# A two-layer hybrid decoder: the low weight parts of the mixers on GpSimd, the convolution's square root used once as a square, the key halves duplicated by DMA

## The chip, the core and the metric

The kernel runs on one core of a Trainium2 chip. The time is the device time of one execution in microseconds (us). Engines are named as the profile does: PE is TensorE's matmul, PEld its weight load, DVE is VectorE, ACT is ScalarE, POOL is GpSimd, and SP is SyncE, which here issues every DMA.

## The reference

Two layers over x of 1024 tokens by 1024 channels, all in float32. What matters of it:

```python
for l in range(DEPTH):                       # 2
    h = rmsnorm(x, attn_norm[l])
    proj = h @ w_in[l]                       # 1024 x 1952
    (c_q, c_kv, k_r, g_b, g_c, u_conv, u_pool, q_sw, k_sw, v_sw) = jnp.split(proj, pts, axis=-1)
    y_a = mla_attention(...)                 # latent attention, 4 heads, causal
    y_b = short_gated_conv(g_b, g_c, u_conv, conv_w[l])   # g_b * conv3(g_c * u)
    y_c = multiscale_pool(u_pool, pool_w[l], pool_scale[l])
    y_d = swa_sink_attention(...)            # window 128, 4 heads on 2 key heads
    groups = jnp.stack([y_a, y_b, y_c, y_d], axis=2)      # each scaled to unit mean square
    ...
    x = x + mixed @ w_o[l]
    h2 = rmsnorm(x, ffn_norm[l])
    gate, up = jnp.split(h2 @ w_gate_up[l], 2, axis=-1)
    x = x + (jax.nn.silu(gate) * up) @ w_down[l]
return rmsnorm(x, final_norm)
```

## The kernel before

Activations lie transposed in SBUF: 128 channels on the partitions, 512 tokens (one of two halves, `t`) along a row. A float32 product is made of matmuls in `fp32r`: each operand is split into a high part, a cast that ACT makes, and a low part, the operand minus its high part, which DVE makes; then high times high, high times low and low times high are summed in PSUM (`mm3`, L260). So each weight tile that is loaded costs an ACT cast and a DVE subtraction before PE can use it.

The first stage of a layer is the mixers. `expect_layer` lists the weights in the order of their use: 15 column tiles of `w_in` (1024 columns each; in layer 0 three of them are made elsewhere), a narrow one for the rotary key, and 8 tiles of `w_o` (768 columns). `weights` loads one (L194), casts it (L202) and subtracts (L203), into a ring of two pairs of slots; `ahead` and `take` keep one set fetched. The narrow weights of the latent attention (128 or 256 columns) go through the same function with buffers of their own (`vraw`, `vhi`, `vlo`). `project` takes a set and makes both halves of one column tile of the input projection. The root-mean-square norm is not applied to the input of the projection but to its output: every product leaves PSUM multiplied by `r_of(t)`, the reciprocal root of the mean square, by `mul_to` (L359 whatever calls it).

The convolution (`conv`) takes three projections for each of two channel tiles: `u` and `g_c`, whose product `z` is filtered with three taps on ACT and DVE (L711, L713), and `g_b`, which gates the result. The windowed attention holds each key head twice, on partitions 0 to 63 and 64 to 127, with a high and a low tile each (`kk`), because the low part of a query lies in the other half of the partitions; L539 to L542 make them, and L573 are the first matmuls that read them. Its sixteen units (`swa_unit`) are laid between the projections by `swa_some`. In the latent attention `mix_values` transposes probabilities (L1032) and multiplies them with the values (L1044); the last block of a diagonal needs a strip of zeros that GpSimd clears (L1041). In the mixers GpSimd makes only those clears and 8 additions a layer for feed-forward weights (`premake`, L749 to L752).

After the mixers come the output projection (`out_part`, `out_last`), the entrance to the feed-forward part (`combine`, the splits of the first gate weights, L283), 22 steps of gate and up, and the down projection. There GpSimd makes sums of weights (L1213 to L1243, L1532) and the product of the gate (L1454).

The order of instructions on every engine is not that of the code. `Order` takes the traced program with a cost for each instruction and plans it by list scheduling, forth and back; `impose` then fixes each engine's order, and the planned ends choose the eight PSUM banks. Its rule on DVE and GpSimd stands in `run`: an instruction of DVE with two wide inputs in SBUF is stretched by `SHARED` = 0.6 of what it overlaps with GpSimd's, and the other way round.

Of the kernel before, what the change touches and what calls it, by code (L numbers as in the profile page):

```python
# [14 lines left out]
AF = mybir.ActivationFunctionType  # L15
ALU = mybir.AluOpType
AX = mybir.AxisListType

P = 128
# [92 lines left out]
def trunk_kernel(ctx: ExitStack, tc: tile.TileContext, ins, out, given=None):  # L112
    nc = tc.nc
    act, dve, pe, pool, sp = nc.scalar, nc.vector, nc.tensor, nc.gpsimd, nc.sync
# [9 lines left out]
    R, F = View(slots, F32R), View(slots, F32)  # L124

    def rd(ap):
        return ap.bitcast(F32)
# [42 lines left out]
    def tmp(tag="te"):  # L170
        return tpool.tile([P, HT], F32, name=tag, tag=tag, bufs={"te": 2, "tn": 3, "tp": 3}[tag])
# [7 lines left out]
    def ring_next():  # L179

        if len(ring) == 2:
            ring_drop()
        ring.append((R.pair(), R.pair()))
        return ring[-1]
# [5 lines left out]
    def weights(src, n):  # L190
        if n > 2 * P:
            s = F.pair()
            raw = F.ap2(s)
            sp.dma_start(raw[:, :n], src)  # L194
            hi, lo = (R.ap2(i) for i in ring_next())
            F.free_pair(s)
        else:
            raw = wpool.tile([P, 2 * P], F32, name="vraw", tag="vraw")
            sp.dma_start(raw[:, :n], src)
            hi = wpool.tile([P, 2 * P], F32R, name="vhi", tag="vhi")  # L200
            lo = wpool.tile([P, 2 * P], F32R, name="vlo", tag="vlo")
        act.copy(hi[:, :n], raw[:, :n])  # L202
        dve.tensor_tensor(out=lo[:, :n], in0=raw[:, :n], in1=rd(hi[:, :n]), op=ALU.subtract)  # L203
        return hi, lo

    def rope_weights(l):
# [17 lines left out]
    def expect_layer(l):  # L224
        for m in (2, 3, 0, 4, 5, 6, 1, 13, 14, 10, 11, 12, None, 7, 8, 9):
            if m is None:
                expect(rope_weights, l)
            else:
                if l or m not in (2, 3, 0):
                    expect(weights, ins["w_in"][l, m], 2 * HT)  # L230
        for d in range(NK):
            expect(weights, ins["w_o"][l, d, :, 2 * P :], 6 * P)
# [58 lines left out]
    def half_split(f, gain=None):  # L291
        h, l = R.half(), R.half()
        split(R.ap(h), R.ap(l), f, gain)
        return h, l
# [63 lines left out]
    def mul_to(o, a, b):  # L358
        dve.tensor_tensor(out=o, in0=a, in1=b, op=ALU.mult)  # L359

    def pcol(l, c, rows=slice(0, P)):
        return par[rows, l * PC_N + c : l * PC_N + c + 1]
# [55 lines left out]
    for l in range(L):  # L418
# [20 lines left out]
        def project():  # L439
            w = take()  # L440
            pp = [proj(w, t) for t in range(2)]
            ahead()
            return pp

        def r_of(t):
            return F.ap(ratt[t])
# [26 lines left out]
        if l == 0:  # L473
# [12 lines left out]
            raw = F.pair()  # L486
# [22 lines left out]
            for i in range(L):  # L509
                for o, c, n in ((nsink, PC_SINK, 4), (nffn, PC_FFN, NK)):  # L510
                    dve.tensor_scalar(
                        out=o[:, i * n : i * n + n],
                        in0=par[:, i * PC_N + c : i * PC_N + c + n],
# [20 lines left out]
        for t in range(2):  # L534
            f = tmp()
            mul_to(f, pk[t], r_of(t))
            for g, own, oth in ((0, hd, tl), (1, tl, hd)):
                k1, k2 = R.ap(kk[g][0] + t), R.ap(kk[g][1] + t)
                act.copy(k1[own], f[own])  # L539
                act.copy(k1[oth], f[own])  # L540
                dve.tensor_tensor(out=k2[own], in0=f[own], in1=rd(k1[own]), op=ALU.subtract)
                dve.tensor_tensor(out=k2[oth], in0=f[own], in1=rd(k1[own]), op=ALU.subtract)  # L542
        vs = [[R.half(), R.half()] for _ in range(2)]
        for t in range(2):
            f = tmp()
# [5 lines left out]
            for g in range(2):  # L551
# [3 lines left out]
                    out=o[:, :, 1, :], in0=pv[:, :, g, :], in1=rd(o[:, :, 0, :]), op=ALU.subtract  # L555
# [140 lines left out]
        def conv(ct):  # L696

            z = F.pair()
            pp = project()
            for t in range(2):  # L700
                mul_to(F.ap(z + t), pp[t], r_of(t))
            yield
            pp = project()
            for t in range(2):
                f = tmp()
                mul_to(f, pp[t], r_of(t))
                mul_to(F.ap(z + t), F.ap(z + t), f)
            ac = F.pair()
            zf, af = F.ap2(z), F.ap2(ac)
            c = PC_CONV + ct  # L710
            act.activation(af, zf, AF.Copy, scale=pcol(l, c + 4))  # L711
            for lag, tap in ((1, c + 2), (2, c)):
                dve.scalar_tensor_tensor(  # L713
                    out=af[:, lag:],
                    in0=zf[:, : S - lag],
                    scalar=pcol(l, tap),
                    in1=af[:, lag:],
                    op0=ALU.mult,
                    op1=ALU.add,
                )  # L720
            F.free_pair(z)
            yield
            pp = project()
            for t in range(2):
                f = tmp()
                mul_to(f, pp[t], r_of(t))
                mul_to(F.ap(ac + t), F.ap(ac + t), f)
            y["b"][ct] = [ac, ac + 1]
            yield

        for _ in conv(0):
            swa_some(3)
# [5 lines left out]
        raw = wpool.tile([P, 2 * P], F32, name="vraw", tag="vraw")  # L738
# [23 lines left out]
        for ct in range(2):  # L762
            pp = nextp
# [17 lines left out]
            else:  # L781
# [7 lines left out]
                out=dst,  # L789
                in0=src,  # L790
                scalar=cst[:, CC_INVW + ct : CC_INVW + ct + 1],
                in1=uf,
# [8 lines left out]
            for t in range(2):  # L801
                h, lo = half_split(dst[:, t * HT : (t + 1) * HT])
# [20 lines left out]
        for m in range(2):  # L823
            pp = project() if m else nextp
            for t in range(2):
                f = tmp()
# [6 lines left out]
        pp = project()  # L833
# [12 lines left out]
        for t in range(2):  # L846
# [14 lines left out]
            f = tmp()  # L861
# [24 lines left out]
        def values():  # L886

            wv = weights(ins["w_ukv"][l, :, 2 * P :], 2 * P)
            for jj in range(4):
                va[jj] = [R.half(), R.half()]  # L890
# [428 lines left out]
        def snap(p):  # L1319
            o = tmp("tn")  # L1320
            act.copy(o, p)  # L1321
            return o
# [12 lines left out]
        steps = ((0, 0), (0, 1), (1, 0), (1, 1), (2, 0), (2, 1), (3, 1), (3, 0))  # L1335
        pieces = (0, 3, 2, 3, 1, 1, 1, 1)
        conv1 = conv(1)
        next(conv1)
        group_scale("d")
# [276 lines left out]
        for f in range(3, NFF):  # L1616
# [22 lines left out]
            k2 = snap(w.pa)  # L1639
# [96 lines left out]
        for n, (c, m) in enumerate(units):  # L1736
            if n + 2 < len(units):
                raws.append(dn_raw(*units[n + 2]))
            if c in fresh:
                u, t = fresh[c]  # L1740
# [460 lines left out]
```

## Time and profile before

| | |
|---|---|
| median of 3 runs | 2062.73 us (2062.2 to 2065.04) |
| span of the profiled execution | 2061.2 us |
| instructions in it | 26597 |
| granted clock of TensorE | 0.998 |
| busy share of the span: PE, PEld, DVE, ACT, POOL | 99%, 81%, 73%, 48%, 28% |

The profile gives the span, from the first to the last instruction, of one execution; no device time of its own stands beside it. The median of the runs is 1.5 us above that span. The mixers take from the start to about 350 us and from about 1075 to 1375 us, the gate and up steps from about 475 and 1490 us, the down projections from about 820 and 1840 us. In the views, a row of instructions names line, engine, operation, the tiles written and read (buffer numbers left out), their shapes and how many there are; then the busy time, the mean of one in ns, and the idle time of the engine ahead of it with what ended it. In a timeline the first two numbers are the start and the length in us. Slots are all named `u`.

### The profile page before, as it was taken

The page shows a single profiled execution, that of the slowest core. Times are in us where ns is not written, and L with a number is a line of the kernel's source. Part 1 is how long each engine was busy: PE and PEld are TensorE (multiplying, and loading weights), DVE is VectorE, ACT ScalarE, POOL GpSimd, SP SyncE. Part 2 cuts the span into 40 slices and gives each one's busy share as a digit, 9 for nine tenths or more (in the row PEclk, how much of TensorE's full clock was granted, in tenths as well). Part 3 has the DMA queues.
Part 4 walks back from the last instruction along what each step waited for, and adds up shares of the span by engine and source line. Part 5 has one row for each costly group of instructions (what it writes and reads, how often), then busy time and mean ns, then how long its engine had stood idle before and what let it go on. Part 6 is the DMA issues. An engine that isn't in the chain of part 4 may idle for free.

```text
span 2061.2 us, 26597 instructions
## 1 busy us (share of the span) xinstructions
PE 2035.3 (99%) x9422; PEld 1673.6 (81%) x9422; DVE 1503.7 (73%) x2443; ACT 992.6 (48%) x1743; POOL 577.3 (28%) x420
## 2 busy tenths in 40 slices
PE   9999999999999999999999999999999999999998
PEld 7887888778888888888888878888788877788887
DVE  8779979987666667655657898889866655585555
ACT  7447657753333334444433666668433333354342
POOL 0200000037777773000002000000577777710000
PEclk9999999999999999999999999999999999999999
DMA  5211223334554556766413112142455555487642
GB/s 191 90 57 46 84 78 96 137 133 168 181 175 167 189 169 235 265 220 208 140 46 124 37 42 97 61 144 94 159 169 178 178 175 170 154 302 237 204 171 96
DMA packets 142118, 302.37 MB, mean 147 GB/s; under 512 B 13856, under 2 KB 60960, under 8 KB 141984
## 3 DMA queue, kind: packets, MB, share of 16 engines
q1 hardware_dynamic: 141984, 300.66, 43.1%
q8 instruction: 74, 1.21, 0.2%
q14 instruction: 60, 0.49, 0.1%
HBM read 212.00 MB, written 87.56 MB: 145 GB/s over the span
## 4 chain that ended last, share of the span: by engine, by line
PE 68%; POOL 7%; DVE 5%; DMA 4%; issue 2%; ACT 2%; SPq 0%; DVEq 0%; POOLq 0%; ACTq 0%
PE ps_mm L260 25%; PE ps_s L260 21%; PE ps_t L260 8%; PE ps_pv L260 6%; POOL u L1532 3%; PE ps_pv L1044 2%; PE ps_t L1032 1%; DMA u<-in_w_dn 1%; POOL tp L1454 1%; DMA ad<-u 1%; POOL u L1214 1%; DVE u L283 1%; POOL u L1213 1%; ACT u L280 1%; DMA u<-in_w_gu 1%
## 5 line engine op out<-in xcount | busy, mean ns | idle before, releaser
L260 PE MATMUL ps_mm<-u,u 128*128 128x512 f32 (+1 forms) x3378 | 831.0, 390 | 3.4 <-ACT u L280 2.3
L260 PEld LDWEIGHTS ps_mm<-u,u 128*128 128x128 f32 x3378 | 615.4, 188 | 130.4 <-issue 5.3
L260 PE MATMUL ps_s<-u,u 128*128 128x512 f32 x2670 | 636.1, 390 | 5.8 <-DVE tn L352 2.3
L283 DVE TENSOR_TENSOR u<-u,u 128x1024 fp32r<-128x1024 f32 (+2 forms) x400 | 443.3, 1126 | 225.2 <-ACT u L280 173.4
L260 PEld LDWEIGHTS ps_s<-u,u 128*128 128x128 f32 x2670 | 499.5, 188 | 117.8 <-ACT tn L1321 3.9
L280 ACT CAST u<-u 128x1024 fp32r<-128x1024 f32 (+2 forms) x400 | 345.1, 881 | 505.4 <-POOL u L1215 60.1
L260 PE MATMUL ps_t<-u,u 128*128 128x512 f32 (+1 forms) x1124 | 255.3, 378 | 2.8 <-DVE u L1447 2.7
L260 PEld LDWEIGHTS ps_t<-u,u 128*128 128x128 f32 x1124 | 201.6, 188 | 45.8 <-DVE u L1447 6.5
L1454 POOL TENSOR_TENSOR tp<-tp,u 128x512 f32<-128x512 f32 x80 | 135.1, 1689 | 341.7 <-ACT tp L1453 341.7
L260 PE MATMUL ps_pv<-u,u 128*128 128x512 f32 x744 | 177.8, 390 | 1.6 <-DVE te L1658 1.0
L260 PEld LDWEIGHTS ps_pv<-u,u 128*128 128x128 f32 x744 | 139.3, 188 | 32.1 <-ACT tn L1321 1.9
L1041 POOL MEMSET u<- 128x128 f32 x32 | 5.9, 211 | 472.9 <-PE ps_pv L1044 149.3
L1453 ACT ACTIVATE tp<-tp 128x512 f32<-128x512 f32 x80 | 50.5, 631 | 155.2 <-DVE tp L359 155.1
L749 POOL TENSOR_TENSOR u<-u,u 128x512 f32<-128x512 f32 x4 | 6.0, 1509 | 380.4 <-PE ps_t L622 288.9
L1532 POOL TENSOR_TENSOR u<-u 128x352 f32<-128x352 f32 x64 | 80.5, 1259 | 31.6 <-DMA u<-in_w_dn 30.2
L280 ACT CAST u<-ps_t 128x512 fp32r<-128x512 f32 (+3 forms) x132 | 65.1, 504 | 48.1 <-PE ps_t L1032 26.7
L1532 POOL TENSOR_TENSOR u<-u,u 128x352 f32<-128x352 f32 x64 | 85.0, 1328 | 3.0
L285 ACT ACTIVATE u<-u,par 128x512 fp32r<-128x512 f32 x100 | 70.6, 717 | 28.5 <-DVE u L359 11.1
L283 DVE TENSOR_TENSOR u<-ps_t,u 128x512 fp32r<-128x512 f32 (+3 forms) x132 | 75.9, 582 | 11.1 <-ACT u L280 9.8
L286 DVE SCALAR_TENSOR_TENSOR u<-u,par,u 128x512 fp32r<-128x512 f32 x100 | 73.7, 750 | 5.9 <-ACT u L285 5.9
L324 ACT ACTIVATE tn<-u 128x512 f32<-128x512 f32 (+1 forms) x91 | 52.3, 595 | 48.6 <-DVE u L1723 42.1
L359 DVE TENSOR_TENSOR tp<-tp,u 128x512 f32<-128x512 f32 x76 | 72.5, 954 | 2.0
(208 smaller groups left out, 2359.3 us busy)
## 6 DMA issues: line engine op xcount, KB each, us to landing
u<-in_w_gu SPq DMA_DIRECT2D x92, 512.0 KB, 4.1
ad<-u SPq DMA_DIRECT2D x154, 256.0 KB, 3.9
u<-ad SPq DMA_DIRECT2D x70, 512.0 KB, 5.1
u<-in_w_dn SPq DMA_DIRECT2D x64, 352.0 KB, 3.4
qd<-u SPq DMA_DIRECT2D x64, 352.0 KB, 2.4
u<-qd SPq DMA_DIRECT2D x32, 512.0 KB, 4.7
u<-in_w_in SPq DMA_DIRECT2D x28, 512.0 KB, 3.5
u<-in_w_dn SPq DMA_DIRECT2D x24, 512.0 KB, 5.2
```

Source lines behind the costliest of these rows:

```text
L260: pe.matmul(o, w, r, start=start and k == 0 and i == 0, stop=stop and k == n - 1 and i == 2, skip_group_check=again,)
L280: a = act.copy(hi, f)
L283: dve.tensor_tensor(out=lo, in0=f, in1=rd(hi), op=ALU.subtract)
L285: a = act.activation(hi, f, AF.Copy, scale=gain)
L286: dve.scalar_tensor_tensor(out=lo, in0=f, scalar=gain, in1=rd(hi), op0=ALU.mult, op1=ALU.subtract)
L324: act.activation(q, f, AF.Square)
L359: dve.tensor_tensor(out=o, in0=a, in1=b, op=ALU.mult)
L1032: pe.transpose(p[:, b * P : (b + 1) * P], pr[b][j // 4][:, (j % 4) * P : (j % 4 + 1) * P], ident,)
L1044: pe.matmul(py[:, c0:], v_of(j, h), R.ap(s)[:, c0:], start=j == 0 and n == 0, stop=j == nj - 1 and n == 1,)
L1453: last_silu = act.activation(g, g, AF.Silu)
L1454: pool.tensor_tensor(out=g, in0=g, in1=r, op=ALU.mult)
L1532: pool.tensor_tensor(out=o, in0=a, in1=b, op=ALU.add)
```

## The change

Three edits. In `weights`, the subtraction of a tile of more than 256 columns goes to GpSimd, and the narrow ones stay on DVE. In the windowed attention's keys, the second half of each pair is no longer computed from the product but copied from the first half by DMA. In the convolution, ACT writes the square of `r_of(t)` into `z`, the product of `u` is multiplied with it, and that of `g_c` then with `z`, so that one multiplication for each half goes and one tile of `tmp` with it.

```diff
@@ weights
         act.copy(hi[:, :n], raw[:, :n])
-        dve.tensor_tensor(out=lo[:, :n], in0=raw[:, :n], in1=rd(hi[:, :n]), op=ALU.subtract)
+        low = pool if n > 2 * P else dve
+        low.tensor_tensor(out=lo[:, :n], in0=raw[:, :n], in1=rd(hi[:, :n]), op=ALU.subtract)
@@ keys of the windowed attention
                 act.copy(k1[own], f[own])
-                act.copy(k1[oth], f[own])
                 dve.tensor_tensor(out=k2[own], in0=f[own], in1=rd(k1[own]), op=ALU.subtract)
-                dve.tensor_tensor(out=k2[oth], in0=f[own], in1=rd(k1[own]), op=ALU.subtract)
+                for k in (k1, k2):
+                    sp.dma_start(rd(k[oth]), rd(k[own]))
@@ conv
             for t in range(2):
-                mul_to(F.ap(z + t), pp[t], r_of(t))
+                act.activation(F.ap(z + t), r_of(t), AF.Square)
+                mul_to(F.ap(z + t), pp[t], F.ap(z + t))
             yield
             pp = project()
             for t in range(2):
-                f = tmp()
-                mul_to(f, pp[t], r_of(t))
-                mul_to(F.ap(z + t), F.ap(z + t), f)
+                mul_to(F.ap(z + t), pp[t], F.ap(z + t))
```

In the changed file every line from L203 to about L700 stands one further down: L203 becomes L204, L260 L261, L283 L284, L359 L360, and the transfers of the keys are L543. The planner runs again over the changed program, so that the order moves in the mixers and at the entrances; from some 475 us on, and again from some 1490 us, the order on PE is what it was.

GpSimd, from the program's start into the mixers of layer 0 (`u_...` are tiles; their numbers differ by a few between the two programs). Before, its first work is the additions for feed-forward weights:

```order
L749 TENSOR_TENSOR u_1031<-u_1030,u_1029 128x512
L749 TENSOR_TENSOR u_1043<-u_1042,u_1041 128x512
L750 TENSOR_TENSOR u_1043<-u_1042,u_1041 128x512
L750 TENSOR_TENSOR u_1031<-u_1030,u_1029 128x512
L751 TENSOR_TENSOR u_1042<-u_1043,u_1041 128x512
L751 TENSOR_TENSOR u_1030<-u_1031,u_1029 128x512
```

and now:

```order
L204 TENSOR_TENSOR u_430<-u_427,u_429 128x1024
L204 TENSOR_TENSOR u_707<-u_704,u_706 128x1024
L204 TENSOR_TENSOR u_551<-u_548,u_550 128x1024
L204 TENSOR_TENSOR u_873<-u_870,u_872 128x1024
L204 TENSOR_TENSOR u_1003<-u_1000,u_1002 128x1024
L204 TENSOR_TENSOR u_1165<-u_1162,u_1164 128x1024
L749 TENSOR_TENSOR u_1029<-u_1028,u_1027 128x512
L750 TENSOR_TENSOR u_1029<-u_1028,u_1027 128x512
```

Six low parts of 1024 columns have moved in ahead of those additions.

GpSimd again, during the latent attention and the output projection of layer 0. Before, only the clears for `mix_values` stand there:

```order
L1041 MEMSET u_2441 128x128 x2
L1041 MEMSET u_2653 128x128 x2
L1041 MEMSET u_2840 128x128 x2
L1041 MEMSET u_3077 128x128 x2
L1041 MEMSET u_3236 128x128 x2
L1041 MEMSET u_3441 128x128 x2
```

and now:

```order
L1041 MEMSET u_2437 128x128 x2
L204 TENSOR_TENSOR u_2493<-u_2490,u_2492 128x768
L1041 MEMSET u_2649 128x128 x2
L1041 MEMSET u_2836 128x128 x2
L204 TENSOR_TENSOR u_2682<-u_2679,u_2681 128x768
L204 TENSOR_TENSOR u_2869<-u_2866,u_2868 128x768
L204 TENSOR_TENSOR u_2918<-u_2915,u_2917 128x768
L1041 MEMSET u_3073 128x128 x2
L1041 MEMSET u_3232 128x128 x2
L204 TENSOR_TENSOR u_3265<-u_3262,u_3264 128x768
L204 TENSOR_TENSOR u_3617<-u_3614,u_3616 128x768
L1041 MEMSET u_3437 128x128 x2
```

Low parts of `w_o` now stand between the clears, two of them ahead of the last pair shown.

SP, the DMA queue, at the keys of the windowed attention in layer 0. Before, weight loads (L194, L199) and feed-forward weights (L747) follow each other:

```order
L194 DMA u_702<-in_w_in 128x1024
L194 DMA u_872<-in_w_in 128x1024
L199 DMA vraw<-in_w_uq 128x256
L747 DMA u_1042<-in_w_gu 128x1024
L199 DMA vraw<-in_w_uq 128x256
```

and now:

```order
L194 DMA u_704<-in_w_in 128x1024
L543 DMA u_433<-u_433 64x512
L543 DMA u_435<-u_435 64x512
L543 DMA u_434<-u_434 64x512
L543 DMA u_436<-u_436 64x512
L194 DMA u_870<-in_w_in 128x1024
L199 DMA vraw<-in_w_uq 128x256
L543 DMA u_433<-u_433 64x512
L543 DMA u_435<-u_435 64x512
L543 DMA u_434<-u_434 64x512
L747 DMA u_1040<-in_w_gu 128x1024
L543 DMA u_436<-u_436 64x512
```

The four tiles of the keys are copied half by half, the first four transfers ahead of the next load of `w_in`.

## The prediction, made before the changed kernel was run

> **What bounds the kernel now.** I read the span and clock first, then the busy time of each engine, then the same by stage, then who ended TensorE's waits.
>
> ```profile
> core 0: 2061.2 us, clock 0.998
> PE 2035.3 (99%) x9422; PEld 1673.6 (81%) x9422; DVE 1503.7 (73%) x2443; ACT 992.6 (48%) x1743; POOL 577.3 (28%) x420
> ```
>
> TensorE (PE) is busy in all but 25.9 us of the span, and the clock is full: nothing is to be had from the clock, and no more than those 25.9 us from waits, apart from delays that the modelled ends of matmuls hide. By stage (PE, PEld, DVE, ACT, POOL busy, in this order):
>
> ```profile
> 25.00:350.00 325.00, 323.07 (x1610) 265.20 (x1608) 282.26 (x656) 196.03 (x448) 13.91 (x24) 1.00 0.21 71
> 350.00:475.00 125.00, 120.23 (x525) 96.81 (x524) 111.74 (x154) 78.88 (x120) 31.91 (x19) 1.00 0.40 140
> 1075.00:1375.00 300.00, 299.37 (x1509) 247.65 (x1508) 259.33 (x617) 179.66 (x419) 14.65 (x24) 1.00 0.22 74
> 1375.00:1490.00 115.00, 112.08 (x488) 90.70 (x487) 104.81 (x143) 73.57 (x110) 34.16 (x19) 1.00 0.40 139
> ```
>
> The two long stretches are the mixers of layers 0 and 1, where the edits lie: VectorE (DVE) is busy for 87% and 86% of them, yet PE is idle for only 1.93 and 0.63 us. GpSimd (POOL) is nearly free there. The two short stretches are the entrances to the feed-forward part, with 4.77 and 2.92 us of PE idle. The waits:
>
> ```profile
> PE ps_s L260 <- DVE tn L352: 2.3, 1, 2.3
> ...
> PE ps_pv L634 <- DVE u L283: 0.8, 1, 0.8
> ...
> PE ps_mm L260 <- DVE u L203: 0.3, 1, 0.3
> ```
>
> The longest is at the entrance; in the mixers one of 0.8 us leads, and the low parts that move (L203) cost PE 0.3 us in the whole span.
>
> **The change part by part.** The rows that price it:
>
> ```profile
> L203 DVE TENSOR_TENSOR u<-u,u 128x1024 fp32r<-128x1024 f32 (+1 forms) x43 | 49.1, 1145 | 22.8 <-PE ps_t L260 10.8 <-PE ps_mm L260 8.2 <-ACT u L202 2.1
> L359 DVE TENSOR_TENSOR te<-ps_mm,u 128x512 f32<-128x512 f32 x39 | 26.8, 687 | 16.5 <-PE ps_mm L260 16.2
> L542 DVE TENSOR_TENSOR u<-te,u x8: 685/687/689, 33.9 to 1050.2; 64x512 fp32r<-64x512 f32 x8
> L540 ACT CAST u<-te x8: 617/619/621, 31.5 to 1049.4; 64x512 fp32r<-64x512 f32 x8
> L324 ACT ACTIVATE tn<-u x91: 399/618/648, 9.2 to 2047.2; 128x512 f32<-128x512 f32 x79, 128x256 f32<-128x256 f32 x12
> L749 POOL TENSOR_TENSOR u<-u,u x4: 1289/1502/1742, 91.7 to 1115.7; 128x512 f32<-128x512 f32 x4
> ```
>
> Off VectorE: the 43 wide low parts, 49.1 us (27 of 1024 columns, 16 of 768); 8 key copies of L542, 8 x 0.687 = 5.5 us; in the convolution, per channel tile and half, two products become one, 8 x 0.687 = 5.5 us over both layers. Together 60.1 us of 541.6 in the two mixer stretches.
>
> ScalarE: 8 copies of L540 leave (8 x 0.619) and 8 squares come (8 x 0.618): nothing. A square needs only the root's factor, long made, so it can stand ahead of its product; its cover is the projection's matmuls.
>
> GpSimd: a 512-column subtraction or addition takes 1.289 us when it is alone, 2.52 ns a column, so 2.58 us for 1024 and 1.93 us for 768: 27 x 2.58 + 16 x 1.93 = 100.5 us of new work. That it has time for them is not the question; what it does to VectorE meanwhile is. GpSimd and VectorE in the entrance of layer 0:
>
> ```profile
> 449.00 1.74 POOL L1243 TENSOR_TENSOR u<-u 128x512 f32<-128x512 f32 x1
> 450.70 1.74 POOL L1454 TENSOR_TENSOR u<-u,u 128x512 f32<-128x512 f32 x1
> ```
>
> ```profile
> 449.51 1.78 DVE L1447 SCALAR_TENSOR_TENSOR u<-u,u 128x512 f32<-128x512 f32 x1
> 451.21 0.68 DVE L1447 SCALAR_TENSOR_TENSOR u<-ps_s,u 128x512 f32<-128x512 f32 x1
> ```
>
> The VectorE instruction with both inputs in SBUF starts inside GpSimd's, ends at 451.29, 0.55 us after GpSimd's end at 450.74, and takes 1.78 us; the same with one input in PSUM takes 0.68. GpSimd's next one, issued at 450.70, takes 1.74 instead of 1.29. They take turns by whole instructions. A subtraction of 2.58 us therefore blocks VectorE by 0 (nothing of that kind comes) to 2.58 us.
>
> The Trainium skill, "SBUF — State Buffer", section "SBUF: two separate sides", says the same in other words: the port pair that the two share is an exclusive lock, held for a whole instruction, and the loser blocks fully. These rows agree with it, and by that rule alone the move would be weighed by VectorE's blocked time, not by GpSimd's idle time; that is the slower rival below.
>
> Two places of the mixers of layer 0 where a low part is wanted soon (cast, VectorE, PE):
>
> ```profile
> 206.19 1.03 ACT L202 CAST u<-u 128x1024 fp32r<-128x1024 f32 x1
> 243.29 0.84 ACT L202 CAST u<-u 128x768 fp32r<-128x768 f32 x1 [0.24 <-DVE u L286]
> ```
>
> ```profile
> 207.38 0.68 DVE L359 TENSOR_TENSOR u<-u,te 128x512 f32<-128x512 f32 x1
> 207.98 1.22 DVE L203 TENSOR_TENSOR u<-u,u 128x1024 fp32r<-128x1024 f32 x1
> 209.11 0.75 DVE L286 SCALAR_TENSOR_TENSOR u<-u,par,u 128x512 fp32r<-128x512 f32 x1
> 244.63 0.95 DVE L203 TENSOR_TENSOR u<-u,u 128x768 fp32r<-128x768 f32 x1
> 245.50 0.76 DVE L986 CUSTOM_DVE_ANT_0 ps_s<-ps_s,cst,sm 128x512 f32<-128x512 f32 x1
> ```
>
> ```profile
> 209.55 0.85 PE L260 MATMUL ps_mm<-u,u 128*128 128x512 f32 x3
> 245.64 1.67 PE L260 MATMUL ps_mm<-u,u 128*128 128x512 f32 x6 [0.32 <-DVE u L203]
> ```
>
> At the first, GpSimd could begin when L359 ends at 208.06 and would hold to 210.64; L286, at 209.11, would lose 1.5 us. At the second it would run from 244.13 to 246.06, beside L986 that works in PSUM: no loss. The mean of the two, 0.75 us, times 43 is 32 us (ends 0 and 43 x 2.58 = 111). VectorE's balance is then -60.1 + 32 = -28 us, 5% of its work in the mixers.
>
> What of it reaches PE. *Gains*: (a) PE idle in the mixers is 1.93 + 0.63 = 2.56 us; I take half, -1.3. (b) At the entrances no instruction changes, and VectorE is as full there as before; only what is left over from the mixers could come sooner: ends 0 and -7.7, I take -1.0, near the end that the unchanged work speaks for. (c) Delays too short for the wait view: bounded by the visible 2.56, I take -1.0. *Losses*: (d) blocked VectorE. The mixers hold one sample of it, the additions for the feed-forward weights:
>
> ```profile
> 94.42 2.97 POOL L750 TENSOR_TENSOR u<-u,u 128x512 f32<-128x512 f32 x2
> ```
>
> ```profile
> 94.48 1.78 DVE L466 TENSOR_TENSOR u<-te,u 64x512 fp32r<-64x512 f32 x1 [0.69 <-ACT u L464]
> 96.29 0.69 DVE L283 TENSOR_TENSOR u<-ps_t,u 128x512 fp32r<-128x512 f32 x1
> ```
>
> ```profile
> 97.04 0.62 PE L634 MATMUL ps_pv<-u,u 128*128 128x256 f32 x3 [0.83 <-DVE u L283]
> ```
>
> L466 is held to 96.26, L283 behind it in VectorE's queue comes late, and PE waits 0.83 us: the longest wait of the mixers is GpSimd's doing. GpSimd is busy 13.91 + 14.65 = 28.6 us in the two stretches, and PE lost 0.83 to it; 100.5 us would cost 2.9 (ends 0, and 6.0 by layer 0 alone). The planner's rule stretches instructions for this sharing (`SHARED`), so part will fall where nobody waits: I take half, +1.5. (e) Late low parts: PE uses the first one at 210.01 (the third matmul of its row) and could have it at 210.64, +0.6; the second at 245.64 against 246.06, +0.4. Two such places a layer make +2.0 at most, 0 at least; PE has other matmuls to put there, and I take +0.6.
>
> The key halves: 16 transfers of 128 KB on SP. Rows of the last low key, of the first scores, of layer 1's, and of the transfer of that size that the kernel has:
>
> ```profile
> 43.70 0.69 DVE L542 TENSOR_TENSOR u<-te,u 64x512 fp32r<-64x512 f32 x1
> 1050.21 0.69 DVE L542 TENSOR_TENSOR u<-te,u 64x512 fp32r<-64x512 f32 x1
> ```
>
> ```profile
> 52.44 0.56 PE L573 MATMUL ps_s<-u,u 128*128 128x128 f32 x4
> L573 PE MATMUL ps_s<-u,u x17: 220/283/283, 1072.7 to 1089.9; 128*128 128x256 f32 x13, 128*128 128x128 f32 x4
> L873 SPq DMA_DIRECT2D u<-u x8: 461/461/536, 181.5 to 1205.0; - x8
> DMA to landing us min/median/max: 2.2/2.3/3.0
> ```
>
> From 43.7 to 52.4 and from 1050.2 to 1072.7 there are 8 and 22 us, and four issues of 0.46 with a landing of 2.3 need 4.1: nothing, covered by the convolution's projections. In layer 0 the next weight load stands behind four of them on SP and cannot start before the low keys of the first half are made; three sets of weights stand ahead of it for PE to work through. If that cover went, PE would wait at L573 for at most those 4.1 us.
>
> The clears (L1041) now queue behind subtractions on GpSimd, and the matmuls of the last diagonal block wait for them:
>
> ```profile
> 331.73 0.35 POOL L1041 MEMSET u<- 128x128 f32 x2 [32.71 <-PE ps_pv L1044]
> 332.73 0.35 PE L1044 MATMUL ps_pv<-u,u 128*128 128x256 f32 x1
> ```
>
> Here 0.65 us lie between; a 1.93 us subtraction in front could cost 1.3. I take nothing and keep it for the range.
>
> Sum: -1.3 - 1.0 - 1.0 + 1.5 + 0.6 = -1.2 us on a span of 2061.2, so 2060.0; the median of the runs lies 1.5 above that span, hence 2061.5.
>
> **The rivals.** *Faster.* The relief lets the order close the gaps: half of the visible 2.56 + 7.69 = 10.25 us, as much again in short delays, little blocked: -5 to -8, 2055 to 2058. For it: 87% VectorE in the mixers. Against: PE idles 1% there. *Slower, by the lock.* Term (d) at 6.0, (e) at 2.0 with a late clear of 1.3, no gain: +5 to +9, 2068 to 2072. It decides once PE loses over (4.1 + 3.3) / 43 = 0.17 us for each subtraction. For it: the 0.83 us above; against: layer 1's additions cost PE nothing visible, its stretch idling 0.63 us in all. *No relief.* VectorE gets back in blocked time all that it gave (1.4 us for each subtraction, near the 1.5 of the first place): 2062 to 2063, no change.
>
> **How the numbers follow.** A change under 0.2% (4.1 us) can't be told from none here. The sum's own case 0.34 (2059 to 2065) and no relief 0.12 make the same 0.46; faster 0.32; slower 0.22, as half of that sample and no late clear already bring it near. The range runs from 2055.5, past most of the faster case, to 2067.5, into the slower one, leaving out about 2 in 10.
>
> **What would show it.** Right: POOL L204 with x43 near 2.6 and 1.9 us; VectorE some 28 us less busy over the two stretches; its instructions with two SBUF inputs lengthened there; PE idle within 3 us of before in each. Wrong to the slow side: PE waits that name POOL L204 or L1041, or a row like L466 at several places. Wrong to the fast side: the entrances' idle cut by half or more.

## The result, and the profile after

The changed kernel takes 2081.65 us (median of 4 runs, 2079.8 to 2084.06); the kernel before took 2063.89 us beside it (2062.2 to 2065.23). The ratio is 1.0084, 95% interval 1.0072 to 1.0096: 17.8 us slower, outside the predicted range. The profiled execution has a span of 2078.4 us, 17.2 us over the one before. The busy line of its page, and the two mixers and two entrances by stage (columns as before):

```profile
PE 2044.4 (98%) x9422; PEld 1676.2 (81%) x9422; DVE 1489.1 (72%) x2384; ACT 991.1 (48%) x1743; POOL 673.7 (32%) x463
```

```profile
25.00:350.00 325.00, 317.32 (x1550) 258.08 (x1549) 265.69 (x614) 190.47 (x437) 56.07 (x39) 0.99 0.23 74
350.00:475.00 125.00, 122.56 (x541) 99.15 (x540) 112.56 (x159) 81.98 (x128) 27.87 (x20) 0.99 0.37 129
1075.00:1375.00 300.00, 294.57 (x1467) 241.18 (x1466) 246.71 (x588) 172.35 (x410) 49.02 (x36) 1.00 0.21 70
1375.00:1490.00 115.00, 114.04 (x510) 92.27 (x509) 106.85 (x153) 79.09 (x125) 21.01 (x17) 1.00 0.36 125
```

TensorE idles in the two mixers for 7.68 and 5.43 us instead of 1.93 and 0.63. VectorE is 16.6 and 12.6 us less busy in these windows, but that flatters it: the mixers take longer now, so that the same windows hold less of the work, 71 VectorE instructions fewer where the edits removed 59. Over the whole span VectorE's busy time fell by 14.6 us (1503.7 to 1489.1). The moved subtractions themselves take what was forecast, 98.5 us instead of 100.5:

```profile
L204 POOL TENSOR_TENSOR u<-u,u 128x1024 fp32r<-128x1024 f32 (+1 forms) x43 | 98.5, 2293 | 654.5 <-ACT u L202 533.0
```

The entrances changed by 2.3 and 2.0 us to the good, though that is mostly their place in the fixed windows. Visible idle does not hold all of the loss, because the modelled ends of matmuls hide short delays. A second measure does: the time from one matmul's start to the next, less the median that the trace of before has for the same pair of lines and widths. Summed over the two mixers it is 26.7 us before and 43.6 after: 16.9 of the 17.2 us. I call it the mixers' stalls below; read it to within a few us, since it is of one execution each.

Who ended TensorE's waits, the four rows that lead in the mixers (engine and tile, line, what it waited for, us in total, times, longest):

```profile
PE ps_t L623 <- DVE tp L612: 3.8, 3, 1.6
...
PE ps_t L344 <- DVE u L327: 2.4, 2, 2.0
PE ps_t L1032 <- DVE u L284: 1.7, 2, 1.0
...
PE ps_t L1032 <- DVE u L1016: 1.6, 1, 1.6
```

All four name VectorE. No wait of TensorE's matmuls names the GpSimd subtractions or the clears; two of its weight loads name a subtraction, for 0.7 and 0.3 us. But the timeline shows who made VectorE late (start, length):

```profile
32.13 6.00 POOL L204 TENSOR_TENSOR u<-u,u 128x1024 fp32r<-128x1024 f32 x2 [0.78 <-ACT u L202]
33.13 2.78 DVE L541 TENSOR_TENSOR u<-te,u 64x512 fp32r<-64x512 f32 x1
35.94 2.74 DVE L327 SCALAR_TENSOR_TENSOR u<-tn,u 128x512 f32<-128x512 f32 x1
38.73 1.42 PE L344 MATMUL ps_t<-u,ones 128*128 128x512 f32 x2 [1.99 <-DVE u L327]
...
251.22 1.83 POOL L204 TENSOR_TENSOR u<-u,u 128x768 fp32r<-128x768 f32 x1 [21.18 <-ACT u L202]
251.25 1.81 DVE L1009 TENSOR_TENSOR sm<-sm 128x1 f32<-128x1 f32 x1
252.99 0.41 DVE L284 TENSOR_TENSOR u<-ps_t,u 128x256 fp32r<-128x256 f32 x1
253.46 0.33 PE L1032 MATMUL ps_t<-cst,u 128*128 128x128 f32 x1 [0.97 <-DVE u L284]
```

Two VectorE instructions of 0.7 us are held for a whole subtraction each, and TensorE waits 1.99 us. At 251 us the held one is a sum of one column, a step of the softmax; the split L284 behind it in VectorE's queue comes late, and TensorE with it. The same line as a whole, in the trace of before (shortest, median, longest in ns):

```profile
L1009 DVE TENSOR_TENSOR sm<-sm x32: 145/154/161, 234.4 to 1345.8; 128x1 f32<-128x1 f32 x32
```

and after, where the median is the same and the longest is twelve times as long:

```profile
L1009 DVE TENSOR_TENSOR sm<-sm x32: 140/152/1817, 241.7 to 1364.7; 128x1 f32<-128x1 f32 x32
```

Over the two mixers I took every VectorE instruction that ran beside an L204 of GpSimd and subtracted the median of its form with no GpSimd beside it. Of 50 that work in SBUF alone, 23 were lengthened, 18 of them by over 1 us, by 31.6 us together. Of 35 with an operand in PSUM none was lengthened by more than 0.02 us.

### The profile page after: what moved, and what is told of

Read it like the earlier page. It is cut to its first block, busy times and chain, and to the rows that moved or that the text cites. A ratio compares the mean times of both kernels' runs of the same rounds, so it can differ in the third digit from the quotient of the medians.

```text
span 2078.4 us, 26641 instructions
## 1 busy us (share of the span) xinstructions
PE 2044.4 (98%) x9422; PEld 1676.2 (81%) x9422; DVE 1489.1 (72%) x2384; ACT 991.1 (48%) x1743; POOL 673.7 (32%) x463
## 4 chain that ended last, share of the span: by engine, by line
PE 78%; DVE 8%; POOL 5%; DMA 3%; issue 3%; ACT 2%; SPq 0%; DVEq 0%; POOLq 0%; ACTq 0%
PE ps_mm L261 31%; PE ps_s L261 23%; PE ps_t L261 9%; PE ps_pv L261 6%; POOL u L1532 3%; PE ps_pv L1044 2%; DVE u L284 1%; PE ps_t L1032 1%; DMA u<-in_w_dn 1%; DVE u L360 1%; POOL tp L1454 1%; PE ps_pv L635 1%; POOL u L1213 1%; PE ps_s L978 1%; DMA u<-in_w_gu 1%
## 5 line engine op out<-in xcount | busy, mean ns | idle before, releaser
L261 PE MATMUL ps_mm<-u,u 128*128 128x512 f32 (+1 forms) x3378 | 836.9, 391 | 4.9 <-ACT u L281 1.6
L261 PEld LDWEIGHTS ps_mm<-u,u 128*128 128x128 f32 x3378 | 617.3, 189 | 130.4 <-issue 4.2
L261 PE MATMUL ps_s<-u,u 128*128 128x512 f32 x2670 | 636.4, 391 | 3.6 <-DVE tp L1670 1.2
L284 DVE TENSOR_TENSOR u<-u,u 128x1024 fp32r<-128x1024 f32 (+2 forms) x400 | 445.7, 1131 | 221.3 <-ACT u L281 165.2
L261 PEld LDWEIGHTS ps_s<-u,u 128*128 128x128 f32 x2670 | 499.8, 188 | 115.6 <-ACT tn L1321 4.3
L204 POOL TENSOR_TENSOR u<-u,u 128x1024 fp32r<-128x1024 f32 (+1 forms) x43 | 98.5, 2293 | 654.5 <-ACT u L202 533.0
L261 PE MATMUL ps_t<-u,u 128*128 128x512 f32 (+1 forms) x1124 | 257.6, 381 | 2.6 <-DVE u L1447 2.5
L261 PEld LDWEIGHTS ps_t<-u,u 128*128 128x128 f32 x1124 | 202.7, 189 | 46.7 <-DVE u L1447 6.7
L261 PE MATMUL ps_pv<-u,u 128*128 128x512 f32 x744 | 177.4, 390 | 0.6 <-DVE te L1658 0.6
L261 PEld LDWEIGHTS ps_pv<-u,u 128*128 128x128 f32 x744 | 139.5, 188 | 30.7 <-DVE te L1658 1.1
L284 DVE TENSOR_TENSOR u<-ps_t,u 128x512 fp32r<-128x512 f32 (+3 forms) x132 | 74.7, 579 | 22.8 <-ACT u L281 21.6
L325 ACT ACTIVATE tn<-u 128x512 f32<-128x512 f32 (+1 forms) x91 | 52.5, 596 | 48.7 <-DVE u L1723 40.1
L360 DVE TENSOR_TENSOR tp<-tp,u 128x512 f32<-128x512 f32 x76 | 74.0, 974 | 2.0
L1243 POOL TENSOR_TENSOR u<-u 128x512 f32<-128x512 f32 x38 | 71.9, 1893 | 5.9 <-DVE u L284 5.9
```

Source lines behind the costliest of these rows:

```text
L204: low.tensor_tensor(out=lo[:, :n], in0=raw[:, :n], in1=rd(hi[:, :n]), op=ALU.subtract)
L261: pe.matmul(o, w, r, start=start and k == 0 and i == 0, stop=stop and k == n - 1 and i == 2, skip_group_check=again,)
L284: dve.tensor_tensor(out=lo, in0=f, in1=rd(hi), op=ALU.subtract)
L325: act.activation(q, f, AF.Square)
L1243: pool.tensor_tensor(out=q4, in0=q4, in1=F.ap(self.raw[1] + 1), op=ALU.add)
```

## The experiments

Times are medians; the kernel before stood at 2063.5 to 2064.5 us in every group, and ratios are to it. A table at the end has all runs.

**Which edit.** e1_keys_conv is the changed kernel with the subtraction back on VectorE, e2_pool_only the kernel before with that edit alone, e6_keys the kernel before with the key transfers alone.

```diff
# e1_keys_conv, against the changed kernel (e2_pool_only: the reverse, on the kernel before)
-        low = pool if n > 2 * P else dve
-        low.tensor_tensor(out=lo[:, :n], in0=raw[:, :n], in1=rd(hi[:, :n]), op=ALU.subtract)
+        dve.tensor_tensor(out=lo[:, :n], in0=raw[:, :n], in1=rd(hi[:, :n]), op=ALU.subtract)
# e6_keys, against the kernel before
-                act.copy(k1[oth], f[own])
-                dve.tensor_tensor(out=k2[oth], in0=f[own], in1=rd(k1[own]), op=ALU.subtract)
+                for k in (k1, k2):
+                    sp.dma_start(rd(k[oth]), rd(k[own]))
```

> The changed kernel with the low parts of the weights back on VectorE; the key transfers and the square stay. Lock theory (GpSimd's subtractions block VectorE, and PE waits for VectorE): all of the +17 us goes, and the 11 us that these two edits take off VectorE may give a little: 2058 to 2065, ratio to before 0.997 to 1.001. Transfer theory (the 16 key transfers hold up the DMA queue and the first scores): most of the loss stays, 2072 or more. Late-low theory (low parts come later from GpSimd, VectorE is not the matter): 2058 to 2065 as well, so this run does not tell it from the lock.

> The kernel before with only the low parts on GpSimd. Lock theory and late-low theory: 2077 to 2086, as the changed kernel or a little worse, since 11 us less is taken off VectorE. Transfer theory: 2058 to 2066.

> The kernel before with the key transfers alone, old planner. The keys and the square together stood 2.4 us above the kernel before (2066.2 against 2063.9). If the transfers are hidden and the rest is the luck of another order: 2061 to 2066. If the transfers cost what was seen: 2065 to 2068.

2066.16, 2080.74 and 2062.58 us. The moved subtractions carry the loss; keys and square together stand 2.2 us above the kernel before, the transfers alone 0.9 below it, and the square was not run alone. A difference of that size is within what another order does by itself (e14_no_low, below).

**Contention or lateness.** In e3_dummy the low parts stay on VectorE, and GpSimd makes an equal subtraction that nobody reads. In e4_pieces each of the changed kernel's subtractions is made in four pieces.

```diff
# e3_dummy, against the kernel before
         dve.tensor_tensor(out=lo[:, :n], in0=raw[:, :n], in1=rd(hi[:, :n]), op=ALU.subtract)
+        if n > 2 * P:
+            pool.tensor_tensor(out=raw[:, :n], in0=raw[:, :n], in1=rd(hi[:, :n]), op=ALU.subtract)
# e4_pieces, against the changed kernel
-        low = pool if n > 2 * P else dve
-        low.tensor_tensor(out=lo[:, :n], in0=raw[:, :n], in1=rd(hi[:, :n]), op=ALU.subtract)
+        low, step = (pool, n // 4) if n > 2 * P else (dve, n)
+        for c in range(0, n, step):
+            cs = slice(c, c + step)
+            low.tensor_tensor(out=lo[:, cs], in0=raw[:, cs], in1=rd(hi[:, cs]), op=ALU.subtract)
```

> The kernel before, low parts on VectorE as there, and on GpSimd the same subtraction once more behind it, written over the raw weights, which nobody reads any more; only the slot of the raw weights is held longer. Results are unchanged. Lock theory: GpSimd blocks VectorE although nobody waits for its result, and VectorE gets no relief: at least +12 us, 2075 to 2090, with PE waiting for VectorE in the mixers. Late-low theory: no low part is late, so 2061 to 2067.

> The changed kernel with each of GpSimd's 43 subtractions cut into four pieces of 256 or 192 columns, about 0.65 or 0.5 us each. Lock theory: VectorE gets its turn between pieces, an instruction is blocked for at most 0.65 us instead of 2.6, and half or more of the loss comes back: 2066 to 2073. Late-low theory: the whole takes as long or longer, so 2079 to 2086.

2086.72 and 2071.99 us. The unread copy costs 22.8 us with every low part made on VectorE: contention alone can make a loss of this size. Not all of the 22.8 us need be contention, since the copy also holds the weights' tiles longer: two waits of TensorE, 1.9 us together, name the cast L202, which none does in the kernel before. Its timeline has the longest single case:

```profile
39.22 5.65 POOL L205 TENSOR_TENSOR u<-u,u 128x1024 f32<-128x1024 f32 x2 [3.29 <-DVE u L203]
40.19 2.43 DVE L510 CAST e_r<-cst 128x128 fp32r<-128x128 f32 x1
42.55 2.47 DVE L203 TENSOR_TENSOR vlo<-vraw,vhi 128x128 fp32r<-128x128 f32 x1
46.45 0.69 DVE L361 TENSOR_TENSOR te<-ps_mm,u 128x512 f32<-128x512 f32 x1
47.79 0.78 PE L551 MATMUL ps_t<-cst,te 128*128 128x128 f32 x4 [3.85 <-DVE te L361]
```

Two instructions of 128 columns take 2.4 us each, and TensorE, waiting for work further down VectorE's queue, loses 3.85 us. In four pieces GpSimd works longer (135.9 us), but hardly a hold is long; the pieces, and the softmax sum beside them:

```profile
L206 POOL TENSOR_TENSOR u<-u,u x172: 586/737/1902, 28.8 to 1370.8; 128x256 fp32r<-128x256 f32 x108, 128x192 fp32r<-128x192 f32 x64
L1011 DVE TENSOR_TENSOR sm<-sm x32: 140/152/591, 238.6 to 1353.4; 128x1 f32<-128x1 f32 x32
```

By the count used above, some 40 VectorE instructions were lengthened by about 16 us together, 2 of them by over 1 us, and 9.7 of the 17.8 us came back.

**What holds.** e5_memset replaces each subtraction by three memsets of the same tile; the low part of the wide weights is left out.

```diff
-        low = pool if n > 2 * P else dve
-        low.tensor_tensor(out=lo[:, :n], in0=raw[:, :n], in1=rd(hi[:, :n]), op=ALU.subtract)
+        if n > 2 * P:
+            for _ in range(3):
+                pool.memset(rd(lo[:, :n]), 0.0)
+        else:
+            dve.tensor_tensor(out=lo[:, :n], in0=raw[:, :n], in1=rd(hi[:, :n]), op=ALU.subtract)
```

> The changed kernel with each GpSimd subtraction replaced by three GpSimd memsets of the same tile (the low part of the wide weights is left out: it is zero), so that GpSimd is about as long busy per tile (estimate 2 to 2.7 us) but reads nothing. Reading theory (VectorE's two-input instructions are held only while GpSimd reads the SBUF): the loss mostly goes, 2062 to 2070, and two-input VectorE instructions beside a memset keep their usual length; tensor_scalar may still be held. Occupancy theory (any GpSimd instruction on the SBUF holds VectorE): 2076 to 2086, as with the subtraction.

2080.99 us, the occupancy theory's time. But its timeline does not show that theory's mechanism:

```profile
168.97 6.12 POOL L205 MEMSET u<- 128x1024 f32 x6 [15.29 <-DVE sm L610]
169.50 0.73 DVE L290 SCALAR_TENSOR_TENSOR u<-u,par,u 128x512 fp32r<-128x512 f32 x1
170.22 0.86 DVE L615 TENSOR_SCALAR tp<-tp,sm 128x256 f32<-128x256 f32 x1
171.08 3.12 DVE L615 TENSOR_SCALAR tp<-tp,sm 128x256 f32<-128x256 f32 x3
173.31 0.30 PE L626 MATMUL ps_t<-cst,tp 128*128 128x128 f32 x1 [0.58 <-DVE tp L615]
174.12 0.73 DVE L290 SCALAR_TENSOR_TENSOR u<-u,par,u 128x512 fp32r<-128x512 f32 x1
```

L290, with two inputs in SBUF, keeps its 0.73 us beside a memset. L615, a tensor_scalar of the softmax with its 0.35 us, takes 1.04 us each, as long as a memset, and its waits lead TensorE's list:

```profile
PE ps_t L626 <- DVE tp L615: 7.1, 9, 1.6
```

This fits the Trainium skill, "SBUF — State Buffer", section "SBUF: two separate sides", which lets a GpSimd instruction that reads the SBUF exclude VectorE's two-input ones, and any GpSimd instruction exclude VectorE's two-port ones; tensor_scalar is one of those that it says can run in that way. Not all of the 7.1 us is the memsets': at 91 us L615 was held by the feed-forward additions, which this order had put beside it. So the run settles who is held, and not what share of the time a memset costs.

**What the planner knows.** The old planner lets the two engines overlap and stretches a wide VectorE instruction by 0.6 of what it overlaps; it takes small ones (of one or two columns) and tensor_scalar as free. The whole new rule (e8_aware_after on the changed kernel, e9_aware_before on the kernel before, e10_aware_pieces on e4_pieces, e11_aware_keys_conv on e1_keys_conv):

```diff
 # kinds
-        two = op == "TensorTensor" or op == "TensorScalarPtr" and i.is_scalar_tensor_tensor
-        if e == "DVE" and two and len(aps) == 2:
-            return None if any(a.memref.startswith("ps_") for a in aps) else "two"
+        src = [a for a in i.ins if hasattr(a, "memref")]
+        if e == "DVE" and op in ("TensorTensor", "TensorScalarPtr"):
+            return None if any(a.memref.startswith("ps_") for a in src) else "two"
 # run: a "two" of VectorE, and then a "pool" of GpSimd
-                    more = min(max(0.0, min(pool, t + 2 * seen) - t) * self.SHARED, 1.15 * seen)
+                    more = max(0.0, pool - t)
-                    more = min(0.8, max(0.0, two - t) * self.SHARED)
+                    more = max(0.0, two - t)
```

> The changed kernel, but the planner is told the rule that the trace showed: a VectorE instruction of any size whose tensors all lie in the SBUF (two-input ones and tensor_scalar) and a GpSimd two-input instruction never run side by side; whichever is later waits to the other's end (before: only wide two-input ones, and 0.6 of the overlap, capped). Placement theory (the loss comes from softmax steps and other urgent VectorE instructions put beside a subtraction because the planner thought it free): most of the loss goes, 2063 to 2072, and TensorE waits for the softmax lines L609 to L612 and L1009 to L1016 fall below 3 us in all. Capacity theory (VectorE has no room in the mixers whatever the order, every blocked microsecond is lost): 2075 to 2083, like the changed kernel.

> Control for the run with the changed planner: the kernel before with the same new rule in its planner, nothing else. Both theories: there are few GpSimd two-input instructions in the mixers of the kernel before, so 2059 to 2066, no difference of more than 0.2%. If it is faster by more than 4 us, the planner's old rule was costing time already before the change; if it is slower by more than 4, the new rule itself is bad and the other run must be read against this one.

> The changed kernel with each GpSimd subtraction in four pieces of a quarter of the columns (2072 with the old planner), and the planner with the new rule. Placement theory: urgent instructions wait 0.6 us at most and are planned around it, 2061 to 2068. Capacity theory: as with the old planner, 2070 to 2074.

> The changed kernel with the low parts back on VectorE and the whole new rule in the planner. Against the kernel before with the same rule (2049.0) it has only the key transfers and the square; against the changed kernel with that rule (2060.2) it lacks only the moved subtractions. If the subtractions still cost under an informed planner: 2046 to 2052. If the key transfers or the square are what costs: 2056 to 2062.

2060.15, 2049.04, 2050.58 and 2051.66 us. The changed kernel gained 21.5 us, but the control, where I had expected nothing, gained 14.8: the old rule had been costing time all along, in the two long stages after the entrances, where GpSimd works most. Before, and in the control:

```profile
475.00:1000.00 525.00, 523.09 (x2301) 430.82 (x2300) 334.24 (x371) 204.59 (x274) 241.61 (x166) 1.00 0.59 198
1490.00:1820.00 330.00, 327.46 (x1426) 265.96 (x1425) 207.60 (x223) 111.97 (x156) 238.10 (x163) 1.00 0.52 174
```

```profile
475.00:1000.00 525.00, 525.00 (x2318) 434.87 (x2317) 353.20 (x378) 208.00 (x281) 234.19 (x165) 1.00 0.60 200
1490.00:1820.00 330.00, 330.00 (x1457) 273.26 (x1456) 231.85 (x232) 116.75 (x163) 234.00 (x164) 1.00 0.55 184
```

TensorE's idle there, 1.91 and 2.54 us, is gone, and it does 17 and 31 more matmuls in the same time. Read against its controls, the change costs 11.1 us under the informed planner (e9) or 8.5 (e11, which differs by the subtractions alone), against 17.8 and 15.5 under the old one. In four pieces it costs nothing (1.1 us less than e11). So the 2060 alone would have spoken for the placement theory, and the controls correct it: planning recovers less than half. The rest goes with the length of the holds; e8 still has 25 instructions lengthened by about 31 us, 18 of them by over 1 us. The softmax sums are none of them:

```profile
L1009 DVE TENSOR_TENSOR sm<-sm x32: 134/150/161, 238.1 to 1349.3; 128x1 f32<-128x1 f32 x32
```

**Which half of the rule.** e13_wide_only has the two lines in `run` alone, on the changed kernel, and e16_wide_before on the kernel before. e17_small_only adds the held small instructions alone:

```diff
# e17_small_only, against the changed kernel
# behind the old test for "two"
+        src = [a for a in i.ins if hasattr(a, "memref")]
+        if e == "DVE" and op in ("TensorTensor", "TensorScalarPtr"):
+            return None if any(a.memref.startswith("ps_") for a in src) else "small"
# run
+                elif kind[k] == "small":
+                    more = max(0.0, pool - t)
+                    seen, taken = seen + more, taken + more
```

> The changed kernel with half of the new rule in its planner: wide two-input VectorE instructions and GpSimd's two-input instructions never run side by side, but the small ones (128x1, 128x2) and tensor_scalar of the softmax stay free in the plan, as before. Theory that the softmax's held instructions carry the loss: it stays, 2072 to 2082, and TensorE still waits for the lines L612 and L1016. Theory that the wide instructions' misjudged overlap carries it: 2058 to 2066, as with the whole rule (2060).

> The kernel before, its planner with the first half of the rule (wide two-input VectorE instructions and GpSimd's two-input ones never side by side). Control for the changed kernel with that half (2063.7). The two long stages after the mixers gained 14 us of TensorE idle there, and should gain it here: 2048 to 2054. Then the change still costs 10 to 15 us under half of the rule. If 2058 to 2064 instead, the half rule had repaired the change itself.

> The changed kernel, its planner with the second half of the rule alone (small two-input instructions and tensor_scalar of VectorE wait for the end of a GpSimd two-input instruction; the wide ones are priced as before). If the softmax's held instructions carry the loss: 2064 to 2070, that is 10 us or more back with nothing gained in the long stages. If the wide ones carry it: 2076 to 2082. If both share it, 2070 to 2076.

2063.69, 2050.07 and 2086.34 us. The wide half does all of the control's gain; with it the change still costs 13.6 us. The small half alone gains nothing, but it also did not do what it says: the sums were held again, perhaps because the plan's times are off while the wide ones are still priced too low:

```profile
L1009 DVE TENSOR_TENSOR sm<-sm x32: 133/151/1258, 245.0 to 1370.0; 128x1 f32<-128x1 f32 x32
```

So the theory that the softmax's small steps carry the loss is not shown; on top of the wide half they are worth 3.5 us (2063.69 to 2060.15).

**Was there anything to win.** e14_no_low (old planner) and e15_no_low_aware (whole rule) make no low part for the wide weights at all and use the high part in its place. e12_aware_memset is e5_memset with the whole rule and memsets and tensor_scalar kept apart as well.

```diff
# e14_no_low, e15_no_low_aware, against the kernel before
         act.copy(hi[:, :n], raw[:, :n])
+        if n > 2 * P:
+            return hi, hi
# e12_aware_memset, run, one line of it: "one" is tensor_scalar, "mset" the end of a memset
+                    more = max(0.0, (pool if kind[k] == "two" else max(pool, mset)) - t)
```

> The kernel before without any low part of the wide weights: the rounded high part is used in its place (this leaves out 43 subtractions, about 50 us of VectorE, and is otherwise the same work for TensorE). It bounds from above what moving the subtractions off VectorE could win. Theory of relief (the prediction's gains of 3.3 us, or the 2055 to 2058 of its faster rival): 2055 to 2061. Theory that VectorE's room is worth nothing under this order: 2062 to 2066.

> The same with the planner that knows the whole rule, to be read against the kernel before with that planner (2049.0). Theory of relief: 2042 to 2046. No relief: 2047 to 2052.

> The three GpSimd memsets in place of each subtraction (low part of the wide weights left out), with a planner that has the whole rule and one more: a memset on GpSimd and a tensor_scalar on VectorE exclude each other. Theory that instructions held at unplanned places made the 2081 of the memsets: 2047 to 2056, near the kernel without any GpSimd work on the weights. Theory that GpSimd's occupation of the weights' buffers, or its queue, costs by itself: 2060 to 2070.

2072.16, 2052.34 and 2055.96 us. Without 43 subtractions, VectorE 1472.0 us busy instead of 1503.7, neither planner's kernel is faster; under the old one it is even 7.7 us slower than the kernel before, under the new one 3.3 us slower than e9. So no gain from relieving VectorE shows. But the old planner's orders scatter by some 8 us for reasons that no single instruction shows, and that would hide a gain of a few us. The memsets cost 4.3 us over e11 once they are planned for, instead of some 15; why they cost anything then stays open.

All runs (stalls as defined above, in us, of the two mixers and of the stretches 475 to 1000 and 1490 to 1820 us):

| kernel | median us | ratio, 95% interval | mixers | long stages |
|---|---|---|---|---|
| before (profile shown) | 2062.73 | | 26.7 | 9.9 |
| after | 2081.65 | 1.0084 (1.0072 to 1.0096) | 43.6 | 12.7 |
| e1_keys_conv | 2066.16 | 1.0012 (1.0003 to 1.0022) | 29.4 | 10.5 |
| e2_pool_only | 2080.74 | 1.0081 (1.0066 to 1.0096) | 40.1 | 14.3 |
| e3_dummy | 2086.72 | 1.0107 (1.0092 to 1.0122) | 44.6 | 11.9 |
| e4_pieces | 2071.99 | 1.0037 (1.0024 to 1.0051) | 29.4 | 11.7 |
| e5_memset | 2080.99 | 1.0081 (1.0066 to 1.0096) | 37.9 | 11.8 |
| e6_keys | 2062.58 | 0.9998 (0.9988 to 1.0007) | 25.4 | 11.5 |
| e14_no_low | 2072.16 | 1.0043 (1.0026 to 1.0060) | 29.1 | 10.1 |
| e17_small_only | 2086.34 | 1.0103 (1.0087 to 1.0118) | 41.6 | 13.8 |
| e13_wide_only | 2063.69 | 1.0004 (0.9995 to 1.0013) | 36.1 | -1.1 |
| e16_wide_before | 2050.07 | 0.9934 (0.9919 to 0.9948) | 24.9 | -1.3 |
| e8_aware_after | 2060.15 | 0.9981 (0.9971 to 0.9990) | 31.0 | -1.3 |
| e9_aware_before | 2049.04 | 0.9930 (0.9915 to 0.9945) | 25.4 | -1.3 |
| e10_aware_pieces | 2050.58 | 0.9937 (0.9921 to 0.9954) | 26.8 | -0.5 |
| e11_aware_keys_conv | 2051.66 | 0.9940 (0.9923 to 0.9957) | 30.4 | -1.3 |
| e12_aware_memset | 2055.96 | 0.9963 (0.9948 to 0.9977) | 30.1 | -1.1 |
| e15_no_low_aware | 2052.34 | 0.9944 (0.9930 to 0.9959) | 29.1 | -0.6 |

The profiled executions of e8 and e11 lie at opposite ends of their runs (2057.9 to 2062.0 and 2050.8 to 2055.9), so the stalls of that pair are closer than their medians. The fastest kernels have no moved subtraction, or short ones, and the repaired planner: e9 is 14.8 us faster than the kernel before that ran beside it, while the changed kernel was 17.8 us slower than its own.

## Why the prediction was wrong

- **VectorE's balance: right by the lengths, in part by luck.** The prediction put 32 us of blocked time against 60.1 us removed, -28 us. The trace shows 31.6 us held, and the lengths of all VectorE instructions add up to 25.3 us less than before (1644.5 to 1619.2). Busy time, which counts the overlap of neighbours once, fell by 14.6 us. That 32 came so near is luck: it is the mean of two places, 1.5 us and none, with ends of 0 and 111.
- **Term (d), the lock: the step that failed.** It was set at +1.5 with an upper end of 6.0. Measured with the edit alone it is +16.8 (e2), with an unread copy on GpSimd +22.8 (e3). The working scaled one wait by GpSimd's busy time (0.83 us for 28.6 us), though GpSimd's busy time hurts only where VectorE is held. The price belongs to the held time: about 17 us of stalls came with 31.6 us held, 2.3 of them by way of the clock (last section). The trace of before did not give that rate either. L466 alone, held by 1.10 us (1.78 less 0.68) with 0.83 lost, would make 24 us of 32; all seven instructions that GpSimd held in the mixers of before, 5.7 us with the same 0.83 lost, would make 4.6. Why more of each hold reached TensorE after the change is not shown beyond this: 18 of the holds were now over 1 us, against 2 before, and cutting them short took half of the loss away (e4).
- **Halving (d) for the planner's rule: not borne out.** The rule prices a hold at 0.6 of the overlap and nothing for small instructions, where the trace has whole holds, and with it 31.6 us of holds came; repairing it took 7 us off the change's cost (15.5 to 8.5). What the old rule kept away, if anything, no run shows.
- **Gains (a), (b), (c), -3.3 us: none seen.** Leaving the subtractions out altogether gave no gain under either planner (e14, e15), though 3.3 us is less than the orders scatter. By these runs VectorE at 87% was not what TensorE waited for in the sum, only instruction by instruction.
- **Term (e), late low parts, +0.6:** no sign of more. e3, where GpSimd makes no low part, loses more than e2; no matmul waits for L204 on GpSimd, and two weight loads do, for 1.0 us together.
- **Key transfers, squares, clears at nothing: right within what can be told** (e6 -0.9 us, e1 +2.2, the square not run alone; no wait of TensorE names L1041).
- **The rivals.** "Slower, by the lock" came, at a chance of 0.22 and with too small a size: it was to decide from 0.17 us for each subtraction, and the loss is 0.41 (17.8 / 43). Its sign in the profile was named rightly: 18 instructions were held by over 1 us, as L466 was, up to 2.1 us.

## What to carry to other kernels

Work moved to an idle GpSimd is to be priced by the VectorE instructions that it will hold, whole instruction by whole instruction and whatever their size, times the share of such a hold that reaches the bounding engine; a balance of busy times says nothing of it. Do not take that share from a few short holds: here it was 0.83 of 5.7 us before and about 17 of 31.6 after. Cut what must go there into short pieces, and tell a scheduler that the two exclude each other before letting it place anything. And run the scheduler's repair on the unchanged kernel too: here that control was worth more than the change.

## What the hardware showed beyond that

Who is held beside a GpSimd subtraction does not depend on size: sums of 128x1 took 1.82 us instead of 0.15, tensor_scalar of 128x256 up to 2.49 (e2) instead of 0.35, and a cast of 128x128 2.43 (e3) instead of 0.21; reciprocals and everything with an operand in PSUM kept their length.

TensorE's granted clock fell to half, for 3.41 us each time, behind some stretches with much waiting. Around the wait of 1.99 us that ended at 38.73 us, in the trace of the changed kernel by short windows (columns as before; the clock stands third from the end):

```profile
36.00:40.00 4.00, 2.01 (x7) 0.83 (x6) 3.01 (x3) 0.00 (x0) 2.13 (x1) 0.93 0.56 164
40.00:43.00 3.00, 3.00 (x9) 2.36 (x8) 0.76 (x2) 1.86 (x3) 0.00 (x0) 0.52 0.15 43
43.00:47.00 4.00, 4.00 (x21) 3.30 (x20) 1.92 (x4) 2.72 (x5) 0.58 (x1) 1.00 0.03 8
```

There are three such stretches in it, from 39.44, 100.88 and 438.80 us, which cost 1.2, 1.1 and 1.6 us by the steps of the matmuls in them; before has none, and neither has e4_pieces. Two of them lie in the mixers, so 2.3 us of the loss there are the clock's. Their starts lie 18 and 99 times 3.413 us apart, as if the clock were decided on a fixed grid, and in the 3.41 us ahead of each TensorE idled for 1.99, 1.94 and 1.64 us. So 2 us of waiting can cost up to 1.6 us more than itself, though it need not: on the same grid 1.63 us from 1121.5 us were not followed by that, and the kernel before has a wait of 2.3 us without it. The Trainium skill, "TensorE: Matmul & The Clock Gate", section "Part 1: The HAM clock gate (the "warmup" mystery)", has the clock fall after an idle window of about 3.4 us; the length agrees with the 3.41 us here, but windows idle for about half were enough.
